# A hybrid decoder layer on eight cores: weight casts reordered, key/value tiles in pairs, ping-pong row sums

## The chip, the cores and the metric

One Trainium2 chip, all eight NeuronCores (two dies: cores 0 to 3 and 4 to 7). Each core computes half of one of four sequences, with its own copy of the weights; the cores do not talk to each other. The metric is the device time of the slowest core, in microseconds. Names: PE is the matrix engine, PEld its weight loads, DVE VectorE, ACT ScalarE, POOL GpSimd, SP the engine that issues most loads.

Executions fall in two states, fast and slow (of the changed kernel's runs, those up to 10,229 us count as fast, those of 10,256 to 10,293 as slow), and even in fast ones some cores are held back by a lower granted PE clock, mostly in the last stage: in the changed kernel's profiled run (8020 to 10,050 us) cores 2 and 3 show a granted clock of 0.81 there, the other six 0.87 or 0.88, and in the K/V stage all eight 0.86 or 0.87. Two measures are therefore used. The official one is the ratio of fast runs. The second, for differences of a per cent or two, is the span of the *shortest core* of each run, as a median over all runs of a kernel: that core is the one the clock disturbed least, and it repeats within 0.5% in every kernel that was run more than once.

## The reference, cut to what matters

```python
h = rms_norm(x, attn_norm)
proj = h @ w_in            # 1024 -> 5640 columns: gated DeltaNet, b_q, b_k, b_v, two gates
bk = rms_norm(b_k per head, k_norm); bk = apply_partial_rotary(bk, cos, sin)   # same for bq
s  = einsum(bq, bk);  pr = softmax(causal s)       # two softmaxes per head
o_b = einsum(pr[0] - lam * pr[1], b_v)
# ... delta rule branch, gates, w_out, squared-ReLU MLP, per-layer embedding
```

Batch 4, sequence 8192, width 1024. A core holds the keys and values of 8192 tokens (64 tiles of 128) and the queries of 4096 of them (eight groups of 512).

## The kernel before: the parts that the argument touches

The program is a list of operations per engine, each engine strictly in its own order. A helper derives the waits from names of tiles that are read and written.

Start-up. Weights are cast from float32 to bf16 in HBM by DMAs in POOL's queue, eight in flight at most (in the trace eight are issued from 1.54 us on, the ninth waits until 20.77):

```python
for r in range(8):
    DMA("pool", win_b[r*128:(r+1)*128, :], w_in[r*128:(r+1)*128, :], writes=["win_b%d" % r])
WIN = ["win_b%d" % r for r in range(8)]
...                                    # 24 more casts: woa, wob, wout, wpg, wup, wdn, wple, cmask
OP("pool", "tensor_tensor", ["negshift", "phalf"], ["negshift"], ..., op=ALU.pow)   # behind them
...
P.sync_engines()                       # every engine waits for every engine
```

The K/V stage, one tile after another with one set of buffers:

```python
DMA("sp", Wkv[:, :, 0:512], winv[:, :, C_BK:C_BK + 512], reads=WIN, writes=["Wkv"])
...
for t in range(NT):                                            # 64
    load_norm_T(xin[t*128:(t+1)*128, :], "attn_g", hT1, ...)   # square, Ln/Exp, scale, 8 transposes, gain
    for c in range(8):  ...  pb[7] += hT1[:, c].T @ Wkv[:, c, 0:512]       # keys
    for c in range(8):  ...  pb[5] += hT1[:, c].T @ Wkv[:, c, 512:1024]    # values
    OP("act", ... Vt[:, t, :] <- pb5)
    qk_post(7, "k_g", t, KT[...])      # copy, square (POOL), reduce, Ln/Exp, 2 scales, rotary, 4 transposes, copy
```

Attention, per head and key tile of 128, over 512 queries; the row sums of the two softmaxes are kept by two engines:

```python
for c in range(2): matmul S_c;  ACT: ptb = exp(0.125 * S_c + bias)
                   # on the four diagonal tiles: POOL multiplies ptb by a mask
for c in range(2): matmul O_c += V.T @ ptb
for c in range(2):
    le = "dve" if c == 0 else "pool"
    OP(le, "tensor_tensor", [pk, "lacc%d" % c], ["lacc%d" % c], out=lacc[c], in0=lacc[c], in1=ptb[pi], op=ALU.add)
```

## Time and profile before

Sixteen runs of the kernel before, over the rounds with the changed kernel: median 11,381 us (11,243 to 11,439). Over the shortest core of 29 runs on the chips of the experiments: 11,221 us (11,203 to 11,235). The stages on the profiled core, read from the prediction's window table and cut at the first square of the K/V stage:

| stage | us before | what it is |
|---|---|---|
| start-up | 338 | casts, waits for them |
| K/V | 1310 | 64 serial tiles of 20.5 |
| attention | 3860 | 1600 tiles, 32 changes of head |
| delta rule | 3651 | unchanged code |
| output and MLP | 2253 | unchanged code, depends on the clock (0.79 here; 2097 us on a core at 0.86) |

### The profile page before, as it was taken

How to read it: one execution, taken by the hardware profiler on the slowest of the kernel's cores; microseconds unless marked ns; L12 is line 12 of the kernel's file. 1: busy time of each engine (PE TensorE's matmuls, PEld its weight loads, DVE VectorE, ACT ScalarE, POOL GpSimd, SP SyncE). 2: the span in 40 equal slices, each digit the busy share in tenths (PEclk: the TensorE clock that was granted, in tenths of full speed). 3: DMA queues.
4: the chain of work that ended last, by engine and by line, in shares of the span. 5: the costliest groups of instructions: out<-in, count | busy, mean ns of one | idle time of the engine just before them, and what ended most of it. 6: DMA issues, size and time to landing. Idle time of an engine off the chain costs nothing.

```text
span 11412.7 us, 113105 instructions; the slowest of 8 cores (11257.3 to 11412.7 us)
## 1 busy us (share of the span) xinstructions
PE 6453.3 (57%) x27648; PEld 2654.0 (23%) x27648; DVE 5657.3 (50%) x7197; ACT 4201.6 (37%) x7621; POOL 3618.5 (32%) x3278
## 2 busy tenths in 40 slices
PE   0333336556556565656455555555555577777888
PEld 0111111111111111111222323222333233333333
DVE  0222227667667686868555656555555511111111
ACT  0122216456546565656333333333333322222211
POOL 0000007557557576658312111111111111111111
PEclk9655557678778787878666666666666688788777
DMA  9200000000000000000000000000000034333333
GB/s 113 48 26 25 25 28 2 9 9 2 9 9 2 9 2 9 2 8 2 25 15 8 12 12 8 15 10 10 10 11 10 11 120 128 118 119 124 113 117 106
DMA packets 296942, 411.81 MB, mean 36 GB/s; under 512 B 27552, under 2 KB 265120, under 8 KB 295200
## 3 DMA queue, kind: packets, MB, share of 16 engines
q1 hardware_dynamic: 294560, 368.90, 10.3%
q0 software_dynamic: 1744, 35.67, 2.8%
q8 instruction: 245, 4.01, 0.1%
q14 instruction: 393, 3.22, 0.1%
HBM read 415.04 MB, written 60.31 MB: 42 GB/s over the span
## 4 chain that ended last, share of the span: by engine, by line
PE 36%; DVE 25%; ACT 12%; issue 11%; POOL 9%; DMA 3%; another core or an unknown queue 2%; DVEq 1%; ACTq 0%; POOLq 0%; SPq 0%
PE pb L361 36%; DVE arena L361 25%; ACT arena L361 12%; POOL arena L361 9%; DMA arena<-xin 2%; DVEq L141 1%; ACT L361 1%; DMA win_b<-w_in 0%; ACTq L141 0%; DMA arena<-win_b 0%; POOLq L141 0%; SPq L364 0%; DMA arena<-wob_b 0%; POOL wdn_b L364 0%
## 5 line engine op out<-in xcount | busy, mean ns | idle before, releaser
L361 PE MATMUL pb<-arena 128*128 128x512 bf16 (+5 forms) x22912 | 5345.5, 388 | 1839.9 <-ACT arena L361 999.6
L361 POOL TENSOR_TENSOR arena<-arena 128x512 f32<-128x512 f32 (+3 forms) x2368 | 2982.0, 1261 | 5491.5 <-ACT arena L361 3244.1
L361 PEld LDWEIGHTS pb<-arena 128*128 128x128 bf16 (+3 forms) x22912 | 2064.6, 109 | 5119.1 <-issue 4627.5
L361 DVE TENSOR_TENSOR arena<-arena 128x512 f32<-128x512 f32 (+4 forms) x2432 | 2818.0, 1162 | 733.0 <-ACT arena L361 323.6
L361 ACT ACTIVATE arena<-arena 128x1 f32<-128x1 f32 (+6 forms) x2112 | 1009.0, 483 | 2911.1 <-DVE arena L361 2405.6
L361 ACT ACTIVATE arena<-pb 128x512 f32<-128x512 f32 (+3 forms) x1856 | 1022.4, 563 | 2764.2 <-PE pb L361 2621.9
L361 PE MATMUL pb<-identb,arena 128*128 128x128 bf16 x3648 | 488.1, 300 | 2527.7 <-DVE arena L361 2328.1
L361 ACT ACTIVATE arena<-pb,biasC 128x512 bf16<-128x512 f32 x2048 | 1287.0, 686 | 678.9 <-PE pb L361 465.3
L361 DVE TENSOR_TENSOR arena<-pb,arena 128x512 f32<-128x512 f32 (+3 forms) x1024 | 653.2, 653 | 1654.9 <-PE pb L361 1609.3
L361 PEld LDWEIGHTS pb<-identb,arena 128*128 128x128 bf16 x3648 | 335.1, 132 | 2736.5 <-issue 2735.8
L361 ACT ACTIVATE arena<-pb,negshift 128x512 bf16<-128x512 f32 x1152 | 728.1, 684 | 326.3 <-PE pb L361 204.4
L361 PE MATMUL pb<-arena,onesf 128*128 128x512 f32 x576 | 549.9, 1067 | 515.1 <-POOL arena L361 399.6
L361 DVE TENSOR_SCALAR arena<-arena 128x1024 bf16<-128x1024 f32 (+4 forms) x835 | 300.8, 366 | 866.8 <-ACT arena L361 840.4
L361 POOL COPY arena<-arena 128x4 f32<-128x4 f32 (+1 forms) x448 | 115.4, 263 | 1531.0 <-DVE arena L361 1508.3
L361 DVE TENSOR_TENSOR arena<-pb,pvs 128x1024 bf16<-128x1024 bf16 (+1 forms) x320 | 323.6, 1011 | 409.1 <-PE pb L361 376.4
L361 DVE TENSOR_REDUCE arena<-arena 128x8 f32<-128x512 f32 (+1 forms) x128 | 87.8, 686 | 807.2 <-POOL arena L361 807.2
L361 DVE SCALAR_TENSOR_TENSOR arena<-arena,pvs 128x512 f32<-128x512 f32 x576 | 432.6, 751 | 61.5 <-DVE arena L361 1.4
L361 ACT ACT_TABLE_LOAD x129 | 165.5, 1283 | 521.7 <-DVE tmp L361 217.4
L361 PEld LDWEIGHTS pb<-arena,onesf 128*128 128x128 f32 x576 | 145.2, 304 | 812.8 <-issue 812.1
L361 POOL TENSOR_TENSOR arena<-arena,cmaskb 128x512 bf16<-128x512 bf16 x256 | 310.5, 1231 | 11.8 <-ACT arena L361 11.8
L361 POOL TENSOR_TENSOR arena<-arena,cs 128x512 f32<-128x512 f32 x128 | 176.4, 1407 | 433.9 <-ACT arena L361 400.8
L361 DVE RECIPROCAL arena<-pb 128x512 f32<-128x512 f32 x64 | 214.9, 3358 | 121.9 <-PE pb L361 121.9
(61 smaller groups left out, 1271.4 us busy)
## 6 DMA issues: line engine op xcount, KB each, us to landing
arena<-xin SPq DMA_DIRECT2D x192, 512.0 KB, 3.6
arena<-wup_b SPq DMA_DIRECT2D x64, 1024.0 KB, 6.8
arena<-wdn_b SPq DMA_DIRECT2D x64, 1024.0 KB, 6.5
arena<-win_b SPq DMA_DIRECT2D x36, 1024.0 KB, 10.2
arena<-wout_b SPq DMA_DIRECT2D x16, 1024.0 KB, 8.8
arena<-wpg_b SPq DMA_DIRECT2D x16, 1024.0 KB, 5.4
out<-arena SPq DMA_DIRECT2D x32, 512.0 KB, 2.7
win_b<-w_in POOLq DMA_DIRECT2D x8, 1410.0 KB, 61.4
```

The source lines that it names most:

```text
L141: eng.wait_ge(semof(sk), val)
L361: P.op(eng, lambda e: getattr(e, name)(*args, **kw), reads, writes)
```

## The change

Its intent: let the K/V stage start as soon as its own 1024 columns are cast, hide the other casts, fill the waits of one K/V tile with another tile's work, and loosen the row sums. The diff, cut to its core:

```diff
+        for r in range(2):
+            DMA("pool", win_b[r*512:(r+1)*512, C_BK:C_BV+512], w_in[...], writes=["win_kv%d" % r])
+        later = []                       # LATER(...) appends, issue_later(n) issues n of them on POOL
         for r in range(8):
-            DMA("pool", win_b[r*128:(r+1)*128, :], w_in[...], writes=["win_b%d" % r])
+            LATER(win_b[r*128:(r+1)*128, 0:C_BK], w_in[...], writes=["win_b%d" % r])
...                                       # all other casts and the mask: DMA("pool") -> LATER
+        # two buffer sets; p1_pre, p1_mm, p1_copy, p1_body, p1_tail are the tile's work cut in five
+        # cs is the tile of the pair: PSUM banks 6, 7, 5 and 0 for cs 0, banks 3, 4, 2 and 1 for cs 1
-        for t in range(NT): ...
+        for n in range(NP):               # 32 pairs
+            both(p1_copy, n)              # PSUM -> SBUF
+            if n > 0: both(p1_tail, n - 1)    # key transposes of the pair before
+            if n + 1 < NP: both(p1_mm, n + 1) # 32 matmuls
+            zip_run(*pair(p1_pre, n + 2), *pair(p1_body, n))   # norm ahead beside rotary, in lockstep
+            issue_later(min(1, max(0, len(later) - 23)))
...
+            issue_later(3)                # once per attention group
...
-        lacc = [A([128, 512]), A([128, 512])]
+        lacc = [[A([128, 512]), A([128, 512])], [A([128, 512]), A([128, 512])]]
-   out=lacc[c], in0=lacc[c], in1=ptb[pi]
+   out=lacc[c][(j + 1) % 2], in0=lacc[c][j % 2], in1=ptb[pi]
```

One double buffer for x was given up on the way (one x tile per set).

More of the change, by code (lines that the diff above doesn't have):

```diff
@@ L373, in build @@
         DMA("sp", ctxm[:], ctxm_d[:, :], writes=["ctxm"])
-        for r in range(8):
-            DMA("pool", win_b[r * 128:(r + 1) * 128, :], w_in[r * 128:(r + 1) * 128, :], writes=["win_b%d" % r])
-        WIN = ["win_b%d" % r for r in range(8)]
-        DMA("pool", woa_b[:, :], w_o_a[:, :], writes=["woa_b"])
-        DMA("pool", wob_b[:, :], w_o_b[:, :], writes=["wob_b"])
+        for r in range(2):
+            DMA("pool", win_b[r * 512:(r + 1) * 512, C_BK:C_BV + 512], w_in[r * 512:(r + 1) * 512, C_BK:C_BV + 512], writes=["win_kv%d" % r])
@@ new lines, in build, with LATER, issue_later @@
+        later = []
+        def LATER(*args, **kw):
+            later.append((args, kw))
+        def issue_later(n):
+            for _ in range(min(n, len(later))):
+                args, kw = later.pop(0)
+                DMA("pool", *args, **kw)
+        for r in range(8):
+            LATER( win_b[r * 128:(r + 1) * 128, 0:C_BK], w_in[r * 128:(r + 1) * 128, 0:C_BK], writes=["win_b%d" % r])
+        for r in range(8):
+            LATER( win_b[r * 128:(r + 1) * 128, C_GA:C_END], w_in[r * 128:(r + 1) * 128, C_GA:C_END], writes=["win_c%d" % r])
@@ L379, in build @@
+        WIN = ["win_b%d" % r for r in range(8)] + ["win_c%d" % r for r in range(8)]
+        LATER( cmaskb[:].rearrange("p a b -> p (a b)"), cmask_d[:, :], writes=["cmaskb"])
+        LATER( woa_b[:, :], w_o_a[:, :], writes=["woa_b"])
+        LATER( wob_b[:, :], w_o_b[:, :], writes=["wob_b"])
         for r in range(2):
-            DMA("pool", wout_b[r * 512:(r + 1) * 512, :], w_out[r * 512:(r + 1) * 512, :], writes=["wout_b%d" % r])
-            DMA("pool", wpg_b[r * 512:(r + 1) * 512, :], w_pg[r * 512:(r + 1) * 512, :], writes=["wpg_b%d" % r])
+            LATER( wout_b[r * 512:(r + 1) * 512, :], w_out[r * 512:(r + 1) * 512, :], writes=["wout_b%d" % r])
+            LATER( wpg_b[r * 512:(r + 1) * 512, :], w_pg[r * 512:(r + 1) * 512, :], writes=["wpg_b%d" % r])
@@ L382, in build @@
         for r in range(8):
-            DMA("pool", wup_b[r * 128:(r + 1) * 128, :], w_up[r * 128:(r + 1) * 128, :], writes=["wup_b%d" % r])
+            LATER( wup_b[r * 128:(r + 1) * 128, :], w_up[r * 128:(r + 1) * 128, :], writes=["wup_b%d" % r])
         for r in range(8):
-            DMA("pool", wdn_b[r * 512:(r + 1) * 512, :], w_down[r * 512:(r + 1) * 512, :], writes=["wdn_b%d" % r])
-        DMA("pool", wple_b[:, :], w_ple[:, :], writes=["wple_b"])
+            LATER( wdn_b[r * 512:(r + 1) * 512, :], w_down[r * 512:(r + 1) * 512, :], writes=["wdn_b%d" % r])
@@ L388, in build @@
+        LATER( wple_b[:, :], w_ple[:, :], writes=["wple_b"])
         OP("dve", "tensor_copy", ["cs"], ["identb"], out=identb[:], in_=C("ident"))
@@ L394, in build @@
         OP("pool", "memset", [], ["phalf"], phalf[:], 0.5)
-        DMA("pool", cmaskb[:].rearrange("p a b -> p (a b)"), cmask_d[:, :], writes=["cmaskb"])
         OP("dve", "tensor_copy", ["posi"], ["posf"], out=posf[:], in_=posi[:])
@@ L490, in build, with p1set @@
         Vt = A([128, NT, 512], BF16)
-        xtb = [A([128, 1024]), A([128, 1024])]
-        junk = A([128, 1024], BF16)
-        xn = A([128, 1024], BF16)
-        hT1 = A([128, 8, 128], BF16)
-        ssx = A([128, 1])
-        Wqk = {"kf": A([128, 512]), "ksq": A([128, 512]), "ssk": A([128, 8]), "kbb": A([128, 512], BF16), "rt": A([128, 4, 8, 8])}
+        def p1set():
+            return {"xt": A([128, 1024]), "junk": A([128, 1024], BF16), "xn": A([128, 1024], BF16), "hT": A([128, 8, 128], BF16),
+                    "ss": A([128, 1]), "kf": A([128, 512]), "ksq": A([128, 512]), "ssk": A([128, 8]), "kbb": A([128, 512], BF16),
+                    "rt": A([128, 4, 8, 8])}
@@ L497, in build @@
+        set0 = p1set()
+        xtb = [set0["xt"]]
+        junk, xn, hT1, ssx = set0["junk"], set0["xn"], set0["hT"], set0["ss"]
+        Wqk = set0
         mark_kv = apos[0]
         Wkv = A([128, 8, 1024], BF16)
+        set1 = p1set()
         winv = win_b.rearrange("(c p) n -> p c n", p=128)
-        DMA("sp", Wkv[:, :, 0:512], winv[:, :, C_BK:C_BK + 512], reads=WIN, writes=["Wkv"])
-        DMA("sp", Wkv[:, :, 512:1024], winv[:, :, C_BV:C_BV + 512], reads=WIN, writes=["Wkv"])
-        for t in range(NT):
-            load_norm_T(xin[t * 128:(t + 1) * 128, :], "attn_g", hT1, "hT1", xtb, junk, xn, ssx)
-            for c in range(8):
-                OP("pe", "matmul", ["hT1", "Wkv"], ["pb7"], pb[7][:, :], lhsT=hT1[:, c, :], rhs=Wkv[:, c, 0:512], start=(c == 0), stop=(c == 7))
-            for c in range(8):
-                OP("pe", "matmul", ["hT1", "Wkv"], ["pb5"], pb[5][:, :], lhsT=hT1[:, c, :], rhs=Wkv[:, c, 512:1024], start=(c == 0), stop=(c == 7))
-            OP("act", "activation", ["pb5"], ["V%d" % t], out=Vt[:, t, :], in_=pb[5][:, :], func=AF.Copy)
-            qk_post(7, "k_g", t, KT[:, :, t * 128:(t + 1) * 128], "KT%d" % t, Wqk)
+        DMA("sp", Wkv[:, :, 0:512], winv[:, :, C_BK:C_BK + 512], reads=["win_kv0", "win_kv1"], writes=["Wkv"])
@@ new lines, in build, with p1_pre @@
+        DMA("sp", Wkv[:, :, 512:1024], winv[:, :, C_BV:C_BV + 512], reads=["win_kv0", "win_kv1"], writes=["Wkv"])
+        def p1_pre(t, cs):
+            B_ = set0 if cs == 0 else set1
+            tb, kb_, vb_ = (6, 7, 5) if cs == 0 else (3, 4, 2)
+            K_ = lambda n: "p1%s_%d" % (n, cs)
+            xt, ss = B_["xt"], B_["ss"]
+            DMA("sp", xt, xin[t * 128:(t + 1) * 128, :], writes=[K_("xt")])
+            yield
+            OP("act", "activation", [K_("xt")], [K_("junk"), K_("ss")], out=B_["junk"], in_=xt, func=AF.Square, accum_out=ss[:, 0:1])
+            yield
+            OP("dve", "tensor_scalar", [K_("ss")], [K_("ss")], out=ss[:, 0:1], in0=ss[:, 0:1], scalar1=1.0 / 1024, scalar2=EPS, op0=ALU.mult, op1=ALU.add)
+            yield
+            OP("act", "activation", [K_("ss")], [K_("ss")], out=ss[:, 0:1], in_=ss[:, 0:1], func=AF.Ln)
+            yield
+            OP("act", "activation", [K_("ss")], [K_("ss")], out=ss[:, 0:1], in_=ss[:, 0:1], func=AF.Exp, scale=-0.5)
+            yield
+            OP("dve", "tensor_scalar", [K_("xt"), K_("ss")], [K_("xn")], out=B_["xn"], in0=xt, scalar1=ss[:, 0:1], scalar2=None, op0=ALU.mult)
+            yield
+            tp = pbf(tb)
+            for c in range(8):
+                OP("pe", "transpose", [K_("xn")], ["pb%d" % tb], out=tp[:, c * 128:(c + 1) * 128], in_=B_["xn"][:, c * 128:(c + 1) * 128], identity=identb[:])
+            yield
+            OP("dve", "tensor_tensor", ["pb%d" % tb, "pvs"], [K_("hT")], out=B_["hT"], in0=tp.rearrange("p (c t) -> p c t", c=8),
+               in1=PVv("attn_g").unsqueeze(2).to_broadcast([128, 8, 128]), op=ALU.mult)
+            yield
@@ new lines, in p1_mm @@
+        def p1_mm(t, cs):
+            B_ = set0 if cs == 0 else set1
+            tb, kb_, vb_ = (6, 7, 5) if cs == 0 else (3, 4, 2)
+            K_ = lambda n: "p1%s_%d" % (n, cs)
+            xt, ss = B_["xt"], B_["ss"]
+            for c in range(8):
+                OP("pe", "matmul", [K_("hT"), "Wkv"], ["pb%d" % kb_], pb[kb_][:, :], lhsT=B_["hT"][:, c, :], rhs=Wkv[:, c, 0:512], start=(c == 0), stop=(c == 7))
+            for c in range(8):
+                OP("pe", "matmul", [K_("hT"), "Wkv"], ["pb%d" % vb_], pb[vb_][:, :], lhsT=B_["hT"][:, c, :], rhs=Wkv[:, c, 512:1024], start=(c == 0), stop=(c == 7))
@@ new lines, in p1_copy @@
+        def p1_copy(t, cs):
+            B_ = set0 if cs == 0 else set1
+            tb, kb_, vb_ = (6, 7, 5) if cs == 0 else (3, 4, 2)
+            K_ = lambda n: "p1%s_%d" % (n, cs)
+            xt, ss = B_["xt"], B_["ss"]
+            kf, ksq, ssk, kbb, rt = B_["kf"], B_["ksq"], B_["ssk"], B_["kbb"], B_["rt"]
+            OP("act", "activation", ["pb%d" % kb_], [K_("kf")], out=kf, in_=pb[kb_][:, :], func=AF.Copy)
+            OP("act", "activation", ["pb%d" % vb_], ["V%d" % t], out=Vt[:, t, :], in_=pb[vb_][:, :], func=AF.Copy)
@@ new lines, in p1_body @@
+        def p1_body(t, cs):
+            B_ = set0 if cs == 0 else set1
+            tb, kb_, vb_ = (6, 7, 5) if cs == 0 else (3, 4, 2)
+            K_ = lambda n: "p1%s_%d" % (n, cs)
+            xt, ss = B_["xt"], B_["ss"]
+            kf, ksq, ssk, kbb, rt = B_["kf"], B_["ksq"], B_["ssk"], B_["kbb"], B_["rt"]
+            OP("pool", "tensor_tensor", [K_("kf")], [K_("ksq")], out=ksq, in0=kf, in1=kf, op=ALU.mult)
+            yield
+            OP("dve", "tensor_reduce", [K_("ksq")], [K_("ssk")], out=ssk, in_=ksq.rearrange("p (g d) -> p g d", g=8), axis=AX.X, op=ALU.add)
+            yield
+            OP("dve", "tensor_scalar", [K_("ssk")], [K_("ssk")], out=ssk, in0=ssk, scalar1=1.0 / 64, scalar2=EPS, op0=ALU.mult, op1=ALU.add)
+            yield
+            OP("act", "activation", [K_("ssk")], [K_("ssk")], out=ssk, in_=ssk, func=AF.Ln)
+            yield
+            OP("act", "activation", [K_("ssk")], [K_("ssk")], out=ssk, in_=ssk, func=AF.Exp, scale=-0.5)
+            yield
+            kf3 = kf.rearrange("p (g d) -> p g d", g=8)
+            OP("dve", "tensor_tensor", [K_("kf"), K_("ssk")], [K_("kf")], out=kf3, in0=kf3, in1=ssk.unsqueeze(2).to_broadcast([128, 8, 64]), op=ALU.mult)
+            yield
+            OP("dve", "tensor_tensor", [K_("kf"), "pvs"], [K_("kf")], out=kf3, in0=kf3, in1=PVv("k_g").unsqueeze(1).to_broadcast([128, 8, 64]), op=ALU.mult)
+            yield
+            kb3 = kbb.rearrange("p (g d) -> p g d", g=8)
+            OP("act", "activation", [K_("kf")], [K_("kbb")], out=kbb, in_=kf, func=AF.Copy)
+            cb = cosT[:, t, :].unsqueeze(1).to_broadcast([128, 8, 8])
+            sn = sinT[:, t, :].unsqueeze(1).to_broadcast([128, 8, 8])
+            x1, x2 = kf3[:, :, 0:8], kf3[:, :, 8:16]
+            OP("dve", "tensor_tensor", [K_("kf")], [K_("rt0")], out=rt[:, 0], in0=x1, in1=cb, op=ALU.mult)
+            OP("dve", "tensor_tensor", [K_("kf")], [K_("rt1")], out=rt[:, 1], in0=x2, in1=sn, op=ALU.mult)
+            yield
+            OP("dve", "tensor_tensor", [K_("kf")], [K_("rt2")], out=rt[:, 2], in0=x2, in1=cb, op=ALU.mult)
+            OP("dve", "tensor_tensor", [K_("kf")], [K_("rt3")], out=rt[:, 3], in0=x1, in1=sn, op=ALU.mult)
+            yield
+            OP("dve", "tensor_tensor", [K_("rt0"), K_("rt1")], [K_("kbb")], out=kb3[:, :, 0:8], in0=rt[:, 0], in1=rt[:, 1], op=ALU.subtract)
+            OP("dve", "tensor_tensor", [K_("rt2"), K_("rt3")], [K_("kbb")], out=kb3[:, :, 8:16], in0=rt[:, 2], in1=rt[:, 3], op=ALU.add)
+            yield
@@ new lines, in p1_tail @@
+        def p1_tail(t, cs):
+            B_ = set0 if cs == 0 else set1
+            tb, kb_, vb_ = (6, 7, 5) if cs == 0 else (3, 4, 2)
+            K_ = lambda n: "p1%s_%d" % (n, cs)
+            xt, ss = B_["xt"], B_["ss"]
+            kbb = B_["kbb"]
+            for h in range(4):
+                OP("pe", "transpose", [K_("kbb")], ["pb%d" % cs], out=pbf(cs)[:, h * 128:(h + 1) * 128], in_=kbb[:, h * 128:(h + 1) * 128], identity=identb[:])
+            OP("act", "activation", ["pb%d" % cs], ["KT%d" % t], out=KT[:, :, t * 128:(t + 1) * 128], in_=pbf(cs)[:, 0:512].rearrange("p (h t) -> p h t", h=4), func=AF.Copy)
@@ new lines, in zip_run, with both, pair @@
+        def zip_run(*gens):
+            gens = list(gens)
+            while gens:
+                for gnr in list(gens):
+                    try:
+                        next(gnr)
+                    except StopIteration:
+                        gens.remove(gnr)
+        NP = NT // 2
+        def both(f, n):
+            for cs_ in range(2):
+                f(2 * n + cs_, cs_)
+        def pair(f, n):
+            return [f(2 * n, 0), f(2 * n + 1, 1)] if n < NP else []
+        zip_run(*pair(p1_pre, 0))
@@ L511, in build @@
+        both(p1_mm, 0)
+        zip_run(*pair(p1_pre, 1))
+        for n in range(NP):
+            both(p1_copy, n)
+            if n > 0:
+                both(p1_tail, n - 1)
+            if n + 1 < NP:
+                both(p1_mm, n + 1)
+            zip_run(*pair(p1_pre, n + 2), *pair(p1_body, n))
+            issue_later(min(1, max(0, len(later) - 23)))
+        both(p1_tail, NP - 1)
         P.barrier()
@@ L568, in emit_pv @@
                     le = "dve" if c == 0 else "pool"
+                    src_l, sk_l = lacc[c][j % 2], "lacc%d_%d" % (c, j % 2)
+                    dst_l, dk_l = lacc[c][(j + 1) % 2], "lacc%d_%d" % (c, (j + 1) % 2)
                     if j == 0:
-                        OP(le, "tensor_copy", [pk], ["lacc%d" % c], out=lacc[c], in_=ptb[pi])
+                        OP(le, "tensor_copy", [pk], [dk_l], out=dst_l, in_=ptb[pi])
                     else:
-                        OP(le, "tensor_tensor", [pk, "lacc%d" % c], ["lacc%d" % c], out=lacc[c], in0=lacc[c], in1=ptb[pi], op=ALU.add)
+                        OP(le, "tensor_tensor", [pk, sk_l], [dk_l], out=dst_l, in0=src_l, in1=ptb[pi], op=ALU.add)
                 if j == J - 1:
@@ L577, in emit_post @@
                 nonlocal obi
-                OP("pe", "matmul", ["lacc0"], ["pb7"], pb[7][:, :], lhsT=onesf[:], rhs=lacc[0], start=True, stop=True)
+                OP("pe", "matmul", ["lacc0_%d" % (J % 2)], ["pb7"], pb[7][:, :], lhsT=onesf[:], rhs=lacc[0][J % 2], start=True, stop=True)
                 OP("dve", "reciprocal", ["pb7"], ["rl"], out=rl, in_=pb[7][:, :])
-                OP("pe", "matmul", ["lacc1"], ["pb7"], pb[7][:, :], lhsT=onesf[:], rhs=lacc[1], start=True, stop=True)
+                OP("pe", "matmul", ["lacc1_%d" % (J % 2)], ["pb7"], pb[7][:, :], lhsT=onesf[:], rhs=lacc[1][J % 2], start=True, stop=True)
                 OP("dve", "tensor_tensor", ["pb2", "rl"], ["o0"], out=o0, in0=pb[2][:, :], in1=rl, op=ALU.mult)
```

## The prediction

> **What bounds the kernel now.** I first cut the span into the program's stages with the view of engines by window, at the times where the chain of waits changes character. Columns: window, length, busy time (and instructions) of PE, PEld, DVE, ACT, POOL, then granted clock, DMA share, GB/s.
>
> ```profile
> 0.00:331.70 331.70, 0.00 (x0) 0.00 (x0) 8.88 (x29) 4.12 (x6) 17.48 (x43) 1.00 0.99 113
> 331.70:1649.00 1317.30, 510.64 (x1792) 209.61 (x1792) 348.94 (x832) 267.01 (x640) 66.44 (x64) 0.59 0.08 27
> 1649.00:5509.00 3860.00, 2192.58 (x7232) 574.92 (x7232) 2793.66 (x2240) 2171.07 (x3552) 2477.13 (x1922) 0.78 0.02 6
> 5509.00:9160.00 3651.00, 1945.52 (x11046) 1080.94 (x11046) 2096.59 (x3500) 1289.08 (x2519) 628.98 (x866) 0.65 0.04 13
> 9160.00:11412.70 2252.70, 1804.59 (x7578) 788.56 (x7578) 409.25 (x596) 470.36 (x905) 428.47 (x384) 0.79 0.37 118
> ```
>
> They are: start-up with the weight casts; keys and values of 64 token tiles; attention; the gated delta rule; output and MLP. Start-up is 99% DMA and no matmul. In the K/V stage no engine is 40% busy: it is bound by latency. The change touches these two and the accumulation in attention; the last two stages (5904 us) keep their code.
>
> Then the timeline of start-up, to see what ends it (start, length, engine, instruction, idle before and releaser):
>
> ```profile
> 20.77 0.52 POOL L364 DMA_DIRECT2D woa_b<-w_o_a  x1 [14.93 <-DMA win_b<-w_in]
> 33.91 0.49 POOL L364 DMA_DIRECT2D wob_b<-w_o_b  x1 [12.62 <-DMA win_b<-w_in]
> ...
> 264.31 0.15 DVE L361 TENSOR_SCALAR negshift<-negshift 128x1 f32<-128x1 f32 x1 [215.10 <-POOL negshift L361]
> ...
> 268.94 62.70 SPq L364 DMA_DIRECT2D arena<-win_b  x2
> 331.69 131.68 SPq L364 DMA_DIRECT2D arena<-xin  x9
> 338.09 1.06 ACT L361 ACTIVATE arena<-arena 128x1024 bf16<-128x1024 f32 x1 [70.52 <-DMA arena<-xin]
> ```
>
> POOL issues all 32 casts in order with eight in flight, so its small `pow` comes at 263.6 us. All engines synchronise on it; only then does SP ask for the K/V weights, and the request spends 62.7 us behind the last casts. Work starts at 338.1.
>
> Last, the chain of waits through one K/V tile (start, length, engine), and a sample of attention's steady state and of its change of head:
>
> ```profile
> 902.15 1.09 ACT arena L361 x2
> 903.41 0.09 issue
> 903.50 1.05 POOL arena L361
> ...
> 909.32 0.60 PE pb L361 x4
> 910.04 0.45 issue
> 910.50 1.15 ACT arena L361 x2
> ...
> 913.60 1.03 PE pb L361 x8
> 914.72 1.24 DVE arena L361
> 915.96 0.14 issue
> 916.09 6.45 PE pb L361 x16
> 922.62 1.09 ACT arena L361 x2
> ```
>
> ```profile
> 3498.66 18.58 POOL L361 TENSOR_TENSOR arena<-arena 128x512 f32<-128x512 f32 x12
> 3499.17 17.06 DVE L361 TENSOR_TENSOR arena<-arena 128x512 f32<-128x512 f32 x11
> ```
>
> ```profile
> 2613.27 3.36 DVE L361 RECIPROCAL arena<-pb 128x512 f32<-128x512 f32 x1 [2.30 <-PE pb L361]
> ...
> 2623.85 0.42 DVE L361 CAST arena<-arena 128x512 f32<-128x512 bf16 x1
> 2624.13 1.04 POOL L361 TENSOR_TENSOR arena<-arena 128x512 f32<-128x512 f32 x1 [10.86 <-DVE arena L361]
> ```
>
> A K/V tile is one serial chain: copies, square, reduce, scale and rotary (902.15 to 909.3), transposes and copy out, the next tile's norm (910.5 to 914.7), transposes, sixteen matmuls, and again: 922.62 - 902.15 = 20.47 us, 64 times, from 338 to about 1648. In attention DVE and POOL run back to back at 1.55 us each, while ACT needs two exponentials of about 0.64.
>
> [...]in the first K/V tile the weight loads come 0.43 us apart for the first thirteen matmuls and about 0.2 apart for the last, and each tile leaves PE mostly idle for 14 us. [...]the same DVE form takes 0.69 us alone in the K/V stage and averages 1.43 in attention[...]. [...]
>
> **The change part by part.** *Start-up.* Only the 1024 K and V columns are cast first, in two pieces of 1024 KB written. Now a 1410 KB piece ends every 13 us (20.77, 33.91, 47.13), so 1024 KB take 9.4; the first piece took 19.2 from issue, so 6.3 of start. The two land at about 1.5 + 6.3 + 18.8 = 26.6 us. The small set-up (sine tables, 10.8 us; the part from the `pow` on, 4.8) fits roughly beside this, as POOL no longer stands in a queue and the positions, which landed late at 38 us behind casts, have less before them. The K/V weights are two loads of 1 MB, 10.2 us each by the issue table, say 15 together; the x tile another 5. First square at about 50 instead of 338: **288 us saved**. The other 40 casts go one per pair of tiles (17 times), then three per attention group (23). Each is 5 to 10 us of DMA where the DMA share is 8% and 2%: no cost, and POOL's 0.49 us per issue is 20 us in all, mostly in its idle time.
>
> *K/V stage.* Two tiles with separate buffers and PSUM banks go in lockstep, with the next pair's norm issued beside this pair's rotary. Work per pair, twice the durations of one tile in the trace: DVE 2 x 5.6 = 11.3 us (norm 0.15 + 0.75 + 1.22, reduce 0.69 + 0.17, scales 2 x 0.69, rotary about 1.3, and gaps), ACT 2 x 4.2 to 4.6, PE 32 matmuls and 24 transposes. What sets the period is the order in the queues. From the end of a pair's matmuls: eight transposes (about 0.8), then DVE does two gain multiplies (2 x 1.3) and only behind them, in its queue, the previous pair's rotary (2 x 1.3), as both were zipped; then PE transposes those keys (1.1), and because these stand ahead of the next matmuls, the next matmuls start at about 0.8 + 2.6 + 2.6 + 0.8 = 6.8 us. The 32 matmuls take 32 x 0.43 = 13.7 cold, 32 x 0.24 = 7.7 warm; with 12 cold ones after a gap of some 4 us, 12 x 0.43 + 20 x 0.24 = 9.9. PE's loop is 16.7. DVE's own loop: from the gain multiplies to the end of the rotary 5.3, then reduces 1.5, a wait for ACT (key copies, then two squares of 1.25) to about 10.7, eight small Ln and Exp at 0.25 until 11.6, two normalisations and four scales 4.7: 15.6. I take 16.4 per pair, in place of 2 x 20.47. Fill (norm of two pairs round the first matmuls) 19 us, drain 14: 19 + 31 x 16.4 + 14 = 541 instead of 1310: **769 us saved**.
>
> *Attention.* The accumulators become ping-pong pairs. An addition still needs the sum before it, so its wait is the same token; it reads two SBUF tensors and writes one as before[...]. At a change of head the other buffer would let the first copy pass the ones-matmul that reads the old sum, but that copy stands in DVE's queue behind both reciprocals, and in POOL's behind the square that waits 10.86 us for DVE. So **0**. The x buffer goes from two to one: a load of 3.6 us against the 14 us and more between a tile's normalisation and the next square, hidden.
>
> Sum: 288 + 769 = 1057 us; 11,405 - 1057 = about **10,350 us**.
>
> **The rivals.** *PE stays cold.* [...] Then the period is 6.8 + 13.7 = 20.5, 31 x 4.1 = 127 us more: 10,475. For it: clock 0.59 throughout this stage now. Against it: matmuls in runs twice as long. *DVE overlaps better than I drew it*, PE stays warm: the floor is DVE's 11.3 plus small waits, say 13: 10,245. Against it: the strict order of the queues. *The late casts get in the way*: an x load beside a cast may wait as the K/V weights did; 10 us in each of 17 pairs would give 170 us back: 10,520. Against it: one cast in flight, not eight. *Ping-pong does help*: if the in-place form is what makes an addition last 1.55 us, attention would fall to ACT's pace of about 1.3 to 1.37, 0.2 x 1600 tiles = 320 us: 10,030. Against it: the in-place scale of the K/V stage takes 0.69, like forms that are not in place. A shift of the phase between DVE and POOL could move attention by some 50 us either way, since the trace shows more than one rhythm there (1.55 at 3500, about 1.62 at 4600).
>
> **Range and chances.** The two large terms are secure: both stages wait, and the waits are taken away. The period (13 to 20.5) moves the sum by about 115 us either way, start-up by 20, attention's rhythm by 50, the slower state of the chip by up to 1%. Range 10,220 to 10,490. For less than 2% to be gained (228 us), more than three quarters of the sum would have to fail: chances 0.98 faster, 0.015 same, 0.005 slower.
>
> **What the new profile would show.** Two casts before the first square, and this at about 50 us (over 80 refutes the start-up step). K/V stage ending near 590 us; periods of 16 to 17 us per pair; PE idle some 4 us before each pair's key transposes, with DVE the releaser; a clock above 0.6. DVE and POOL additions in attention still about 1.43 and 1.3 us on average and the stage within 2% of 3860 (under 3700 refutes the ping-pong step). The last two stages unchanged within 1%. x loads still 3 to 7 us to landing; if ACT waits for them in this stage, the casts do get in the way.

## The result, and the profile after

Changed kernel: median 10,216 us (10,095 to 10,293, 11 runs), against 11,381. The ratio of the fast runs is 0.8965, 95% interval 0.8924 to 0.9007. A ratio compares fast runs of both kernels from the same rounds, so it is not quite the ratio of the medians quoted. The shortest core went from 11,221 to 10,061, 1160 us less. The prediction had said 1055 less (11,405 to 10,350); 10,216 lies just below its range.

The windows of the changed kernel, columns as in the prediction's first table:

```profile
0.00:47.10 47.10, 0.00 (x0) 0.00 (x0) 8.89 (x29) 4.14 (x7) 2.69 (x13) 1.00 0.74 127
47.10:498.00 450.90, 320.36 (x1792) 162.10 (x1792) 318.70 (x832) 234.83 (x640) 74.03 (x81) 0.87 0.37 95
498.00:4359.00 3861.00, 2195.36 (x7232) 575.11 (x7232) 2797.12 (x2240) 2176.06 (x3552) 2486.90 (x1943) 0.78 0.06 13
4359.00:8009.00 3650.00, 1946.25 (x11042) 1079.05 (x11042) 2095.54 (x3500) 1289.66 (x2513) 629.08 (x867) 0.65 0.04 13
8009.00:10206.90 2197.90, 1744.02 (x7583) 774.34 (x7582) 409.47 (x596) 473.89 (x910) 428.29 (x384) 0.82 0.38 121
```

Start-up 338 to 47, K/V 1310 to 451, attention and delta rule the same to 1 us. DVE's 832 instructions in the K/V stage are busy for 319 us in place of 349: the same work, packed. The last stage differs by 55 us, which is the clock column (0.79 before, 0.82 here), not the change: another core of the same run before had 2097 us at 0.86, and one after 2053 at 0.87.

Start-up after, in order of time:

```profile
25.79 0.56 POOL L361 TENSOR_TENSOR negshift<-negshift,phalf 128x1 f32<-128x1 f32 x1 [22.32 <-DVE negshift L361]
...
30.82 7.44 SPq L364 DMA_DIRECT2D arena<-win_b  x2
38.32 100.60 SPq L364 DMA_DIRECT2D arena<-xin  x18
47.09 1.06 ACT L361 ACTIVATE arena<-arena 128x1024 bf16<-128x1024 f32 x1 [17.36 <-DMA arena<-xin]
```

The `pow` that stood at 263.6 us is at 25.8; the K/V weights need 7.4 us in place of 62.7. One period of the paired K/V stage, PE and the DVE and ACT rows that matter:

```profile
90.89 1.05 PE L361 MATMUL pb<-identb,arena 128*128 128x128 bf16 x8 [3.81 <-DVE arena L361]
90.97 2.03 POOL L361 TENSOR_TENSOR arena<-arena 128x512 f32<-128x512 f32 x2 [10.86 <-DVE arena L361]
91.73 8.04 PE L361 MATMUL pb<-arena 128*128 128x512 bf16 x32
92.11 0.69 DVE L361 TENSOR_REDUCE arena<-arena 128x8 f32<-128x512 f32 x1 [1.00 <-POOL arena L361]
...
97.53 1.29 DVE L361 TENSOR_TENSOR arena<-arena 128x512 f32<-128x512 f32 x2
98.74 1.29 DVE L361 TENSOR_TENSOR arena<-arena,pvs 128x512 f32<-128x512 f32 x2
...
99.60 1.06 PE L361 MATMUL pb<-identb,arena 128*128 128x128 bf16 x16
100.32 2.36 DVE L361 TENSOR_TENSOR arena<-pb,pvs 128x1024 bf16<-128x1024 bf16 x2 [0.29 <-PE pb L361]
102.59 0.22 DVE L361 TENSOR_TENSOR arena<-arena,cosT 128x64 f32<-128x64 f32 x1
...
103.69 3.05 ACT L361 ACTIVATE arena<-pb 128x512 f32<-128x512 f32 x6 [2.94 <-DVE arena L361]
...
104.47 1.05 PE L361 MATMUL pb<-identb,arena 128*128 128x128 bf16 x8 [3.81 <-DVE arena L361]
```

The period is 104.47 - 90.89 = 13.6 us for two tiles. Its order is the drawn one: matmuls end at 99.6, transposes, two gain multiplies (100.3 to 102.6), then the rotary of the pair before, then its key transposes (104.5), and only then the next matmuls. PE idles 3.81 us with DVE as releaser. DVE waits for PE only 0.29 us before the gain multiplies, so DVE's own loop is almost as long. A wait that I had not drawn is in the row at 103.69: ACT's key copies wait for the rotary, because they overwrite the key buffer that it reads; POOL's square and DVE's reduce (1.00 us idle) follow from it.

How fast those 32 matmuls ran is read from their weight loads, one per matmul (start, length):

```profile
91.63 0.26 PEld L361 LDWEIGHTS pb<-arena 128*128 128x128 bf16 x2
92.16 0.15 PEld L361 LDWEIGHTS pb<-arena 128*128 128x128 bf16 x1 [0.28 <-issue]
92.59 0.15 PEld L361 LDWEIGHTS pb<-arena 128*128 128x128 bf16 x1 [0.27 <-issue]
...
93.44 0.15 PEld L361 LDWEIGHTS pb<-arena 128*128 128x128 bf16 x1 [0.28 <-issue]
93.78 5.50 PEld L361 LDWEIGHTS pb<-arena 128*128 128x128 bf16 x26 [0.18 <-issue]
```

From the second to the sixth they come about 0.43 us apart, the other 26 about 0.21 (5.50 us together). So each pair does start cold (0.43 us per matmul, against 0.21 warm) after the 3.8 us of idle time, but for about six matmuls and not for the twelve of the prediction. From the third pair on, the slow steps number between 4 and 10 per pair, mostly 5; on this core they are 10 in the 17th and in the 30th pair.

### The profile page after: what moved, and what is told of

Same layout as the page of the kernel before. It is cut to its first block, busy times and chain, and to the rows that moved or that the text cites. A ratio compares the mean times of both kernels' runs of the same rounds, so it can differ in the third digit from the quotient of the medians.

```text
span 10206.9 us, 113389 instructions; the slowest of 8 cores (10056.6 to 10206.9 us)
## 1 busy us (share of the span) xinstructions
PE 6206.0 (61%) x27648; PEld 2590.6 (25%) x27648; DVE 5629.7 (55%) x7197; ACT 4178.6 (41%) x7621; POOL 3621.0 (35%) x3288
## 4 chain that ended last, share of the span: by engine, by line
PE 38%; DVE 25%; ACT 12%; issue 11%; POOL 9%; DMA 4%; DVEq 1%; ACTq 0%; POOLq 0%; SPq 0%
PE pb L361 38%; DVE arena L361 25%; ACT arena L361 11%; POOL arena L361 9%; DMA arena<-xin 3%; ACT L361 1%; DVEq L141 1%; DMA arena<-win_b 1%; ACTq L141 0%; POOLq L141 0%; SPq L364 0%; DMA posi<-pos 0%; SPq L141 0%; DMA oaT_d<-arena 0%; DMA obT_d<-arena 0%
## 5 line engine op out<-in xcount | busy, mean ns | idle before, releaser
L361 PE MATMUL pb<-arena 128*128 128x512 bf16 (+5 forms) x22912 | 5144.9, 378 | 1740.8 <-ACT arena L361 999.5
L361 PEld LDWEIGHTS pb<-arena 128*128 128x128 bf16 (+3 forms) x22912 | 2021.9, 107 | 4865.8 <-issue 4138.4
L361 PE MATMUL pb<-identb,arena 128*128 128x128 bf16 x3648 | 452.1, 287 | 1667.6 <-DVE arena L361 1448.5
L361 DVE TENSOR_SCALAR arena<-arena,pvs 128x512 f32<-128x512 f32 x192 | 93.3, 486 | 353.5 <-ACT arena L361 353.5
```

The source lines that it names most:

```text
L361: P.op(eng, lambda e: getattr(e, name)(*args, **kw), reads, writes)
```

## The experiments

Ten kernels were run. Where a stage's length is given it is read from the profile, from the first load of that stage.

**1. Start-up alone.** The kernel before with the new order of casts; serial tiles and in-place sums stay.

```diff
 (kernel before)
+        casts of K and V columns first, all others LATER
         for t in range(NT):
             ...
+            if t % 2 == 1: issue_later(min(1, max(0, len(later) - 23)))
```

> The kernel before with only the order of the weight casts changed: K and V columns first, the others spread over the K/V stage and attention; the serial K/V tiles and the in-place sums stay. If the two savings are independent, this alone gives the start-up's share read from the two traces: first square at about 47 us in place of 338, so about 290 us less, near 11,090 (ratio 0.974), and the K/V stage stays at 64 x 20.5 = 1310 us. Rival: the late casts disturb the K/V stage or attention and take back 50 us or more.

Measured: ratio 0.9812 (0.9757 to 0.9867), median 11,195; as a verdict at 2% this is "unclear". Shortest core 10,927, so 294 us less, the expected amount. The slowest cores show less, probably because some were held back in each run: the profiled one has cores near 10,935 at clock 0.73 on one die and two of up to 11,106 at 0.72 on the other. First x load at 37.5 us, as in the changed kernel. The late casts take nothing back.

**2. Paired K/V tiles alone.** All casts in front, in-place sums.

```diff
 (changed kernel)
-        LATER(...) / issue_later(...)
+        DMA("pool", ...) for all casts in front, reads=WIN for Wkv
-        ping-pong sums
+        in-place sums
```

> Paired K/V tiles alone: all casts in front as before, in-place sums. If the K/V term is what I mis-sized, this gives about 860 us (1310 to 451 in the traces) and not the 769 of the prediction: near 10,520, ratio 0.924; first square at about 338. Rival: part of the 860 comes from the new start-up, for instance a warmer TensorE; then clearly less, 800 or below.

Measured: ratio 0.9151 (0.9109 to 0.9193), median 10,473; shortest core 10,357, 863 us less. It equals the stage's own shrinkage (1310 - 451 = 859), so the new start-up has no visible part in it. With experiment 1, 294 + 863 = 1157 against 1160 for both: the parts are independent and nothing is left for the ping-pong.

**3. Ping-pong undone.**

```diff
 (changed kernel)
-   out=lacc[c][(j + 1) % 2], in0=lacc[c][j % 2], in1=ptb[pi]
+   out=lacc[c], in0=lacc[c], in1=ptb[pi]
```

> The changed kernel with the ping-pong sums undone. My theory: the same time within 0.3%, attention 3860 us, additions on VectorE 1.43 us and on GpSimd 1.31 as with ping-pong. Rival: ping-pong gives a part of the gain; then 50 us or more slower.

Measured: ratio to the kernel before 0.8913 (0.8871 to 0.8956), shortest core 10,061 us, to the microsecond that of the changed kernel. Attention 3861 us. The costliest groups of attention, changed kernel first, then in place (count | busy us, mean ns of one | idle before):

```profile
L361 DVE TENSOR_TENSOR arena<-arena 128x512 f32<-128x512 f32 x1604 | 2288.4, 1427 | 439.2 <-POOL arena L361 241.6 <-ACT arena L361 48.4 <-DVE arena L361 4.7
L361 POOL TENSOR_TENSOR arena<-arena 128x512 f32<-128x512 f32 x1636 | 2149.8, 1314 | 1322.5 <-ACT arena L361 824.1 <-DVE arena L361 334.3 <-PE pb L361 42.2
```

```profile
L361 DVE TENSOR_TENSOR arena<-arena 128x512 f32<-128x512 f32 x1600 | 2282.5, 1427 | 439.0 <-POOL arena L361 240.4 <-ACT arena L361 49.6 <-DVE arena L361 4.6
L361 POOL TENSOR_TENSOR arena<-arena 128x512 f32<-128x512 f32 x1632 | 2152.9, 1319 | 1293.8 <-ACT arena L361 816.6 <-DVE arena L361 315.6 <-PE pb L361 33.2
```

The point is 1427 ns twice: a second buffer removes no wait where each sum needs the one before it.

**4. Both row sums on DVE.** If not the buffer, what makes an addition last 1.43 us?

```diff
 (changed kernel)
-                    le = "dve" if c == 0 else "pool"
+                    le = "dve"
```

> The changed kernel with both row sums on VectorE, GpSimd keeps masks and squares. If the shared access of VectorE and GpSimd makes an addition last 1.43 us, it falls to about 0.7, two fit under ACT's two exponentials (1.37), and a tile takes about 1.4 in place of 1.6; diagonal tiles (3.8 us now) gain more: attention at 3400 to 3550, total 320 to 450 us less, ratio to the kernel before about 0.86. Rival: the additions are slow in themselves (dependent sums, types); then VectorE needs 2.8 us per tile, attention grows to over 5000 and the kernel is slower than the changed one by 1000 us.

Measured: ratio 0.8474 (0.8419 to 0.853), shortest core 9,527, 534 us less than the changed kernel. Attention 3322 us, better than the 3400 that I had given as the best. The same group in this kernel, and the masks that POOL keeps:

```profile
L361 DVE TENSOR_TENSOR arena<-arena 128x512 f32<-128x512 f32 x3168 | 2142.5, 754 | 67.5 <-POOL arena L361 37.8 <-ACT arena L361 29.3 <-DVE arena L361 0.2
...
L361 POOL TENSOR_TENSOR arena<-arena,cmaskb 128x512 bf16<-128x512 bf16 x256 | 428.2, 1705 | 1816.8 <-ACT arena L361 1816.8
```

DVE does twice the additions in less busy time than before (2142 against 2288 us). DVE and POOL side by side (2288 and 2150 us busy) had cost more than DVE doing both shares. The masks, still on POOL, went from 1.23 to 1.7 us; now DVE makes two additions per tile beside them. That the two engines slow each other is shown by these figures, DVE's addition by 1427 ns beside POOL's against 754 without them. Whether a shared access does it, as the expectation has it, or something else, no run separates.

**5. Half of the K/V matmuls.** Sum over four of eight channel blocks, a wrong result (the comparison reported a relative error of 0.35).

```diff
 (changed kernel, p1_mm)
-            for c in range(8): ... stop=(c == 7)
+            for c in range(4): ... stop=(c == 3)
```

> The changed kernel with sixteen in place of 32 K/V matmuls per pair (the sum over half the channels only, a wrong result on purpose). Theory of two loops nearly in balance: PE's order sets 13.6 us per pair, VectorE's own chain about 13.2 right behind it, so a period of 13.0 to 13.4, K/V stage 430 to 445 in place of 451. Rival, PE alone sets it: 4 us off each of 31 periods, stage about 330. [...]PE's idle stretch grows from 3.8 to about 7 us per pair[...].

Measured (one look): shortest core 10,030, 31 us less; K/V stage 431 us; a period of 219.81 - 206.62 = 13.2 us. Sixteen matmuls less bought 0.4 us per pair, not 4: DVE's loop takes over at once. And the matmuls became slow. PE's rows of one period:

```profile
206.62 1.05 PE L361 MATMUL pb<-identb,arena 128*128 128x128 bf16 x8 [5.71 <-DVE arena L361]
...
207.46 5.77 PE L361 MATMUL pb<-arena 128*128 128x512 bf16 x16
...
213.07 1.06 PE L361 MATMUL pb<-identb,arena 128*128 128x128 bf16 x16
219.81 1.05 PE L361 MATMUL pb<-identb,arena 128*128 128x128 bf16 x8 [5.69 <-DVE arena L361]
```

5.77 us for sixteen is 0.36 each, where 32 took 8.04, 0.25 each. As in the changed kernel, each group starts at 0.43 us per matmul: here for 4 to 12 of 16, there for 4 to 10 of 32. PE's idle stretch grew from 3.8 to 5.7 us and not to 7. The granted clock of the stage is 0.76 against 0.87, still above the 0.59 of the kernel before, because the rest of each group ran at 0.21.

**6. Eight more matmuls per pair**, overwritten by the true sum.

```diff
 (changed kernel, p1_mm)
+            for c in range(4): ... matmul into pb[kb_], start=(c == 0), stop=(c == 3)
             for c in range(8): ... the true keys
```

> Eight more matmuls per pair (their result is overwritten): 2 us more of PE, as much as the cold matmuls that the prediction had put in. If PE's order sets the period, all of it shows: 15.6 us per pair, K/V stage 451 + 31 x 2 = about 513. If VectorE's loop had slack to hide it, less than 480.

Measured (one look): attention starts between 561 and 574 us on the eight cores (491 to 500 in the changed kernel), so the stage grew by about 70 us, 2.3 per pair, more than the 2 expected; the shortest core (10,129) is 68 us longer. On core 1 the 40 matmuls take 10.7 us on average, 2.5 more than the 32 (8.2), as more of them run cold (11 steps of 0.43 us in the pair at 209.42 us; the stage's clock is 0.84 against 0.87), and PE's idle stretch is 3.8 us as before. PE's time converts fully into period: had the matmuls been as cold as I had assumed (1.9 us more), most of my error in this term would not have been one.

**7. K/V stage loosened.** Key buffers doubled over pairs, and the key transposes moved behind the next pair's transposes in PE's queue; the copy to KT one pair later.

```diff
 (changed kernel)
-            kf, kbb = B_["kf"], B_["kbb"]
+            kf, kbb = KF[cs][(t // 2) % 2], KBB[cs][(t // 2) % 2]
         for n in range(NP):
             both(p1_copy, n)
-            if n > 0: both(p1_tail, n - 1)
+            if n > 1: both(p1_tact, n - 2)        # ACT's copy to KT
             if n + 1 < NP: both(p1_mm, n + 1)
             zip_run(*pair(p1_pre, n + 2), *pair(p1_body, n))
+            if n > 0: both(p1_tail, n - 1)        # PE's key transposes
```

> The changed kernel with key buffers doubled over pairs and the key transposes behind the next pair's transposes in PE's queue, so that neither the rotary nor the copies hold the next matmuls. If the two queue orders named in the prediction are what is left, VectorE's 11.0 us of work per pair becomes the bound: period 11.2 to 12.3, K/V stage 380 to 415, 35 to 70 us less in all. Rival: ACT's small operations pace VectorE anyway; then under 15 us.

Measured: ratio 0.8884 (0.8811 to 0.8957), an interval that overlaps the changed kernel's; the shortest core settles it: 9,979 against 10,061, 82 us less. K/V stage 372 us on the profiled core, and DVE is busy 90% of it:

```profile
47.00:418.90 371.90, 292.42 (x1792) 148.26 (x1792) 333.10 (x832) 228.42 (x639) 74.24 (x81) 0.95 0.44 115
```

That is a little more than expected (35 to 70 us; stage 380 to 415), with a period of 11.2. What remained lay in these two queue orders, and the bound is now DVE's work; which of the two gave how much was not tested, as the edit removes both at once. The clock is 0.95: PE's longest idle stretch per pair is now about 2.6 us, and 23 of the 32 pairs have no cold matmul at all.

**8. Masks on DVE too**, K/V stage as changed.

```diff
 (experiment 4)
-                        OP("pool", "tensor_tensor", [pk, "cmaskb"], ...)
+                        OP("dve", "tensor_tensor", [pk, "cmaskb"], ...)
```

> Both row sums and the masks on VectorE, K/V stage as changed. The masks last 1.7 us each on GpSimd beside the sums; on VectorE (two bf16 inputs) at most 0.69, two per diagonal tile, 128 such tiles: 128 x 2 to 2.5 us less than with the sums alone, attention 3322 to about 3020 to 3100. Rival: VectorE becomes the bound in diagonal tiles (2 sums and 2 masks, 2.6 us) and they keep their 3.4: gain under 120 us.

Measured: ratio 0.8302 (0.823 to 0.8375), shortest core 9,362: 165 us less than experiment 4, attention about 3150 to 3160. It lies between the theory (220 to 300) and the rival (under 120), so neither figure was right. I did not separate the cause; DVE with four operations in a diagonal tile is the likely one.

This run showed something else by accident. Its K/V stage has the changed kernel's code, and six cores left it at 493 to 501 us as always, but cores 6 and 7 at 537 and 533. First core 5, then core 7, windows over the stage:

```profile
47.00:498.00 451.00, 322.49 (x1792) 162.25 (x1792) 318.87 (x832) 232.76 (x639) 74.03 (x81) 0.87 0.35 95
```

```profile
47.00:533.00 486.00, 362.30 (x1783) 173.86 (x1780) 316.87 (x828) 231.22 (x632) 74.07 (x81) 0.75 0.34 88
```

and PE's rows of one period on core 7, with four of its weight loads:

```profile
312.02 1.05 PE L361 MATMUL pb<-identb,arena 128*128 128x128 bf16 x8 [3.74 <-DVE arena L361]
312.86 10.15 PE L361 MATMUL pb<-arena 128*128 128x512 bf16 x32
316.28 0.15 PEld L361 LDWEIGHTS pb<-arena 128*128 128x128 bf16 x1 [0.28 <-issue]
316.70 0.15 PEld L361 LDWEIGHTS pb<-arena 128*128 128x128 bf16 x1 [0.28 <-issue]
317.33 0.11 PEld L361 LDWEIGHTS pb<-arena 128*128 128x128 bf16 x1 [0.15 <-issue]
317.59 0.11 PEld L361 LDWEIGHTS pb<-arena 128*128 128x128 bf16 x1 [0.15 <-issue]
322.84 1.22 PE L361 MATMUL pb<-identb,arena 128*128 128x128 bf16 x16
327.80 1.05 PE L361 MATMUL pb<-identb,arena 128*128 128x128 bf16 x8 [3.74 <-DVE arena L361]
```

Here the 32 matmuls take 10.15 us and the period is 15.8, close to the predicted 9.9 and 16.4, but for another reason. Core 7 too starts each pair at 0.43 us per matmul. What differs is the fast part: 0.26 us apart and not 0.21, a factor of 0.82. Besides, of two pairs in a row (at 312.86 and 328.64 us) the first has nine steps of 0.43 us and the second four; their matmuls take 10.15 and 9.33 us.

**9. Late casts not spread.** Undoes one part of the change: K and V columns first, all other casts straight behind them in POOL's queue.

```diff
 (changed kernel)
         P.sync_engines()
+        issue_later(99)
```

> The changed kernel with the other 40 casts not spread: all put into GpSimd's queue in front of the K/V stage, K and V columns still first. Theory: GpSimd stands in line with eight casts in flight until about 310 us, so the first square of keys on GpSimd, which stood at 59 us, comes near 300, and VectorE and PE wait for it: attention starts 200 to 260 us later than 498, the total about 10,300. Rival: only the sixteen DMA engines matter; then the K/V stage loses the waits for x tiles (5 to 10 us per pair in the first 20 pairs, 100 to 200 us) and GpSimd's squares come in time.

Measured (one look): 10,440 us, shortest core 10,350, 289 us more; attention starts at 774 to 802 us on the eight cores. POOL's last cast and its first two key squares, with what DVE does then, and ACT's two longest waits after it:

```profile
291.14 0.49 POOL L364 DMA_DIRECT2D wple_b<-w_ple  x1 [9.47 <-DMA wdn_b<-w_down]
291.65 2.04 POOL L361 TENSOR_TENSOR arena<-arena 128x512 f32<-128x512 f32 x2
292.80 0.69 DVE L361 TENSOR_REDUCE arena<-arena 128x8 f32<-128x512 f32 x1 [150.57 <-POOL arena L361]
...
332.96 1.06 ACT L361 ACTIVATE arena<-arena 128x1024 bf16<-128x1024 f32 x1 [27.50 <-DMA arena<-xin]
364.16 1.06 ACT L361 ACTIVATE arena<-arena 128x1024 bf16<-128x1024 f32 x1 [30.05 <-DMA arena<-xin]
```

The theory's place is right, the first squares come at 291.7 us, and DVE had waited 150 us for them. The size was over the expected 200 to 260, because the rival holds too. Its waits in front of the long one (the first square of x at 104 us in place of 47) are covered by it, but two more follow: ACT waits 57.5 us for x tiles behind the last casts. The key squares came 233 us late (291.7 against about 59), attention 284 on this core. Without the spreading, nearly all of the start-up's gain is lost again.

**10. The gains together:** loosened K/V stage, sums and masks on DVE.

> The two versions that gained put together: loosened K/V stage, sums and masks on VectorE. If independent: K/V stage about 372, attention about 3155, 79 us less than with sums and masks on VectorE alone: near 9,280 on undisturbed cores (those had 9,360), ratio to the kernel before about 0.823. Rival: nothing is independent of the die's clock; 9,360 or more.

Measured: median 9,430 us (9,359 to 9,608), ratio 0.8325 (0.8275 to 0.8375); shortest core 9,279, 83 less than experiment 8, as expected. The expected ratio of 0.823 was missed: it is not below that of experiment 8 (0.8302), and the two intervals overlap. In its rounds the kernel before was faster (11,256 against 11,306 us median), and of its own four fast runs one took 9,447, with cores held back on both dies (up to 9,445 and 9,442 us, both at a mean clock of 0.742). By the shortest core it is 782 us below the changed kernel, and that is 699 (experiment 8) plus 83. It beats both kernels, with a correct result.

## Why the prediction was wrong

The sum was 105 us too small, and one term makes up most of it: the period of the paired K/V stage. By the shortest core the saving was 1160 us.

*Start-up: right.* 288 us predicted, 291 in the traces, 294 alone on the shortest core; first square at 47.1 us against "about 50".

*K/V stage: mechanism right, size wrong.* 769 predicted, 859 measured. "I take 16.4 per pair" was the failing step; it measured 13.6 in the shown period and 13.9 on average (28 periods between 77.37 and 465.46 us in the chain of waits), 31 of them, which is 79 of the 90 us; the rest is the fill and drain, 33 us predicted and about 21 left by the stage's 451. Both parts of the period were too large. The matmuls: "12 cold ones" at 0.43 us and 20 at 0.24 make 9.9 us; about six at 0.43 and 26 at 0.21 were measured, 8.0 us. The slow steps did come back after each gap of 3.8 us, as predicted, but ended sooner. The twelve was my estimate, next to the thirteen of a serial tile before; why they end after six was not tested. The queue order: 6.8 us predicted, 5.7 measured (99.60 to 105.3, where the next matmuls begin). There I had taken gaps between DVE operations from a serial tile, where each waits for the one before: two dependent ones began 0.80 us apart (906.31 and 907.11). In lockstep two tiles alternate and do not wait, and the same form begins 0.60 apart (two in 1.29 us). From the first gain multiply to the key transposes that wait for the rotary it took 4.2 us and not 5.2. DVE's own loop came out at 13.3 instead of 15.6 (13.6 less the 0.29 us that it waits for PE), and I read that from the same gaps; no experiment put the gaps back. Two steps of the working were loose besides: its times for DVE's loop add up to 16.3 from the gain multiplies, and to 15.6 only if the last two are counted from the end of the matmuls; and 16.4 was taken without a reason below PE's own 16.7. Of the signs, these came: DVE as releaser of the key transposes, PE idle about 4 us, clock above 0.6. These did not: periods of 16 to 17 us, and the stage ending near 590 (it ended at 498). The last stage changed by 2.4% and not within 1%, which the clock explains (0.79 before, 0.82 after).

One order I had drawn wrongly without harm: ACT's key copies do not run behind the matmuls but wait for the rotary, as the key buffer is single. Experiment 7 removed it together with the transposes' order.

*Attention: right.* 0 predicted, and experiment 3 gives 0. The reason given, that each sum needs the one before it, fits experiment 3. The prediction had set the 0.69 us of the same DVE form in the K/V stage beside the 1.43 in attention; experiment 4 shows that POOL's additions make the difference: with them out of the way DVE's went from 1427 to 754 ns.

*The rivals.* "PE stays cold" did not happen: pairs started cold (all from the third on) and mostly warmed up after some six matmuls. The 35 us longer stage on two cores of experiment 8 came mostly from another cause, a lower clock of the warm part (on core 7 0.26 us per matmul and not 0.21, the stage's clock 0.75 and not 0.87). "DVE overlaps better than I drew it" is what came true: I gave it 10,245 as a floor and let the range end at 10,220, with PE's order as the reason against; the order was right and its durations were not. The late casts did not get in the way as spread; experiment 9 shows that they would have.

*The baseline.* The prediction subtracted from 11,405, the median of four runs at hand; over sixteen it is 11,381. The profiled run before was a slow one with the last stage at clock 0.79. The difference of 24 us between the two medians is part of the miss, and it had no place in the working.

## What to carry to other kernels

When serial chains are zipped, do not carry over the gaps between an engine's operations: those belong to the waits, and they go with them (here 0.80 us from start to start where the second operation waited for the first, 0.60 where it did not). Walk each engine's queue in program order; it named the right rows here, and what was then left (a single buffer, one transpose placed ahead of matmuls) could be removed for another 82 us. A mean clock has to be read through the single weight loads: 0.87 looked like a warm PE and was mostly five steps of 0.43 us among the 32 of a pair. And before a buffer is doubled, ask whether the wait is for the buffer or for the value; here the second buffer gave nothing, and the gain of 534 us lay in taking POOL's additions from beside DVE's (1427 against 754 ns for one of DVE's).
